# A decoder step on one core: another order of the opening and of the gates and values

## The chip, the cores and the metric

The kernel runs on one core of a Trainium2 chip. The metric is the device time of one execution in microseconds (us); each kernel is run several times and the median counts. A core has five engines that run their own instruction streams and wait for one another by semaphores: TensorE (PE, matmuls and transposes; PEld is its load of weights), VectorE (DVE), ScalarE (ACT), GpSimd (POOL) and SyncE (SP, which issues DMA transfers; ScalarE issues some too).

## The reference

One layer of a decoder, for 1024 prompt tokens and 8 sample tokens, 1032 columns in all, in float32:

```
h    = rmsnorm(x, norm_mix_g)
u, q, k, v, gate, f_low = split(h @ w_in)          # one projection
pool = grouped window means of u (2/4/8/16 tokens) minus u, a linear map, a scale
logf = log_sigmoid(f_low @ w_forget_up + b_forget) / 16
o    = gated linear attention(q, k, v, logf)       # 4 heads, chunks of 64
x    = x + concat(pool, rmsnorm(o) * silu(gate)) @ w_out
mk   = rmsnorm(mem) @ w_km;   mv = rmsnorm(mem) @ w_vm        # 256 memory tokens
x    = x + cross attention(rmsnorm(x), mk, mv) @ w_om
x    = x + square(relu(rmsnorm(x) @ w_up)) @ w_down
```

Its outputs are y, the last rows of u, the state of the attention, and mk and mv.

## The kernel before

Activations are held transposed, features on the partitions and tokens along the row, in chunks of 128 features x 1032 tokens. Each float32 operand of a large product is split into a high and a low part: ScalarE casts the high part (line 159, or 162 with a gain), VectorE or POOL subtracts for the low part (line 160, or 163 with a gain). A product is three matmuls per pair of tiles: high x high, high x low, low x high. A group of projection columns (128 of them) is 8 x 9 = 72 matmuls (gemm_chunk, line 196).

*The opening* (lines 286 to 415) computes the keys of the memory, mk, and prepares the tokens. It is a list of steps in three strings, START_A to START_C, of which each word calls a function with a number:

- m (mem_turn): transposes half of the memory tokens (ptm), multiplies them with a norm vector (mg) and splits them (mn).
- l (k_load): loads a block of 128 columns of w_km in two halves (wkm, 256 KB each) through three raw buffers, and splits them (wk).
- K (k_chunk): a key product, 24 matmuls into acck; e (k_scale) scales it into mkT; t (k_turn) transposes it back (ptk) for the output.
- x (x_load): loads a quarter of the prompt tokens (xt, 1 MB; the fifth is the sample tokens, xs); q (x_square) sums their squares on ScalarE.
- X (x_chunk): transposes a chunk of 128 features of all tokens (ptx), copies it (xT), stores it (xd) and splits it (h); f (f_part): its six matmuls for the low-rank gate (accf).
- S, R, N, r: the norms of the memory and the tokens; L: the gate's weights.

The words set the priority. A scheduler orders each engine's instructions, so that those of later words can pass earlier ones that wait. PSUM has two buffers of the pool mp (acck, ptm, ptk, ptg) and two of accp (ptx, accf, the projection's sums).

*The projection* follows: pool_in(3) (U, line 498, is its scaled copy), forget() (accz, line 465, then Z and Y on VectorE and ScalarE, scans, and decays), pool_in(2), pool_in(1), two groups each of keys and queries, and then gates (g, ge with a reciprocal on VectorE at line 574, gt), values (vt, line 586) and pool_in(0), written out one after the other. pool_win sums windows on POOL (W) and leaves pl on VectorE. Each group also adds pieces of w_down in pairs (ws, line 439), which are ready for the last part of the layer. After the projection comes the recurrence of the attention, again a list of steps: its first need the vt of the last values, kinv and qd; beside them run the products of w_vm (accv, line 732) and of the pooled channels (accp, line 531).

Lines named in the profile: 109 and 103 the gains (norm vectors, loaded as rows grow, transposed as ptg, copied to gcol), 160 splits, 303 the issue of wkm, 345 K, 362 and 364 X, 386 f.

## Time and profile before

| | us |
|---|---|
| times of the kernel before, three runs | 1379.63, 1381.21, 1384.13 |
| median | 1381.21 |
| profiled execution, its time | 1386.28 |
| profiled execution, its span | 1384.6 |

[...] The span begins with the first instruction; all times of rows count from there. The opening ends at about 66.5 us, the projection at about 260 us, and the recurrence follows.

How to read the rows: the page gives the busy time of each engine. In the table of stretches a row is the stretch (from:to in us) and its length, then for PE, PEld, DVE, ACT and POOL the busy us with the number of instructions, then the granted clock, the share of the DMA engines' time in use, and GB/s. In the order in time a row is the start, the duration of all instructions merged in it, the engine, the line, the operation, the tile written and those read, the shape and the count; a bracket gives the idle time of the engine before it and what ended that.

### The profile page before, as it was taken

How to read it: one execution, taken by the hardware profiler on the slowest of the kernel's cores; microseconds unless marked ns; L12 is line 12 of the kernel's file. 1: busy time of each engine (PE TensorE's matmuls, PEld its weight loads, DVE VectorE, ACT ScalarE, POOL GpSimd, SP SyncE). 2: the span in 40 equal slices, each digit the busy share in tenths (PEclk: the TensorE clock that was granted, in tenths of full speed). 3: DMA queues.
4: the chain of work that ended last, by engine and by line, in shares of the span. 5: the costliest groups of instructions: out<-in, count | busy, mean ns of one | idle time of the engine just before them, and what ended most of it. 6: DMA issues, size and time to landing. Idle time of an engine off the chain costs nothing.

```text
span 1384.6 us, 22609 instructions
## 1 busy us (share of the span) xinstructions
PE 1330.3 (96%) x8734; PEld 1237.2 (89%) x8734; DVE 924.0 (67%) x1490; ACT 578.9 (42%) x1060; POOL 135.3 (10%) x177
## 2 busy tenths in 40 slices
PE   7999999899999999999999999989999999989997
PEld 6999999888999999878977898989897999989887
DVE  5778565696555677873768488777867654675664
ACT  6522112355334343543557444445445433232432
POOL 2134100100012000002200011112110000000000
PEclk9999999999999999999999999999999999999999
DMA  7846553585465356565435556556649964986671
GB/s 255 254 142 175 147 148 110 153 251 170 134 193 183 99 176 221 176 226 162 132 116 167 173 192 200 184 169 207 199 163 377 302 214 159 286 245 189 214 223 67
DMA packets 287477, 261.38 MB, mean 189 GB/s; under 512 B 13416, under 2 KB 239602, under 8 KB 287241
## 3 DMA queue, kind: packets, MB, share of 16 engines
q1 hardware_dynamic: 275209, 226.08, 52.8%
q0 software_dynamic: 6400, 21.17, 4.0%
q10 hardware_dynamic: 5760, 12.68, 2.5%
q8 instruction: 68, 1.11, 0.3%
q14 instruction: 40, 0.33, 0.1%
HBM read 195.04 MB, written 64.85 MB: 188 GB/s over the span
## 4 chain that ended last, share of the span: by engine, by line
PE 78%; DVE 7%; DMA 6%; issue 4%; ACT 3%; SPq 0%; POOL 0%; DVEq 0%; ACTq 0%; POOLq 0%
PE acc L196 29%; PE accd L1282 20%; PE acc L1109 16%; PE accl L1282 2%; PE accpv L979 1%; PE acck L345 1%; PE accsc L956 1%; DMA fd<-c 1%; DMA fac<-fd 1%; PE accv L732 1%; DMA w<-in_w_up 1%; PE accg L661 1%; PE psv L913 1%; DMA vt<-in_cache_mem_v 1%; DMA wvm<-in_w_vm 1%
## 5 line engine op out<-in xcount | busy, mean ns | idle before, releaser
L1109 PE MATMUL acc<-T,wuph 128*128 128x260 f32 (+1 forms) x1408 | 290.3, 317 | 10.9 <-DVE c L1153 6.1
L1282 PE MATMUL accd<-F,wdnh 128*128 128x260 f32 (+1 forms) x1344 | 266.0, 310 | 4.5 <-ACT wdnh L159 4.5
L1109 PEld LDWEIGHTS acc<-T,wuph 128*128 128x128 f32 x1408 | 213.8, 190 | 32.1 <-issue 7.3
L1282 PEld LDWEIGHTS accd<-F,wdnh 128*128 128x128 f32 x1344 | 201.1, 189 | 18.5 <-ACT wdnh L159 4.9
L1109 PE MATMUL acc<-T,wupl 128*128 128x260 f32 (+1 forms) x704 | 180.1, 316 | 0.8 <-DVE wupl L160 0.8
L1282 PE MATMUL accd<-F,wdnl 128*128 128x260 f32 (+1 forms) x672 | 167.1, 311 | 3.4 <-DVE wdnl L160 3.4
L1109 PEld LDWEIGHTS acc<-T,wupl 128*128 128x128 f32 x704 | 117.2, 191 | 11.3 <-DVE wupl L160 2.1
L1282 PEld LDWEIGHTS accd<-F,wdnl 128*128 128x128 f32 x672 | 109.5, 189 | 11.6 <-DVE wdnl L160 4.9
L159 ACT CAST wdnh<-wdn 128x1024 fp32r<-128x1024 f32 x52 | 54.5, 1050 | 129.4 <-PE accd L1282 112.4
L196 PE MATMUL acc<-c,womh 128*128 128x260 f32 (+2 forms) x384 | 81.8, 322 | 0.6 <-ACT c L159 0.5
L160 DVE TENSOR_TENSOR wdnl<-wdn,wdnh 128x1024 fp32r<-128x1024 f32 x52 | 63.5, 1221 | 20.7 <-ACT wdnh L159 20.6
L160 DVE TENSOR_TENSOR F<-fac,F 128x1040 fp32r<-128x1040 f32 (+1 forms) x52 | 63.2, 1231 | 15.0 <-ACT F L159 13.2
L159 ACT CAST F<-fac 128x1040 fp32r<-128x1040 f32 (+1 forms) x52 | 54.5, 1056 | 44.7 <-DMA fac<-fd 37.3
L196 PE MATMUL acc<-hm,wqmh 128*128 128x344 f32 x384 | 72.7, 323 | 0.1
L196 PEld LDWEIGHTS acc<-c,womh 128*128 128x128 f32 x384 | 59.5, 188 | 6.6 <-ACT c L159 0.6
L159 ACT CAST wuph<-w 128x512 fp32r<-128x512 f32 x64 | 39.0, 614 | 56.8 <-PE acc L1109 48.2
L196 PEld LDWEIGHTS acc<-hm,wqmh 128*128 128x128 f32 x384 | 61.7, 188 | 1.1 <-DVE v L260 0.4
L1113 ACT ACTIVATE c<-c 128x512 f32<-128x512 f32 (+1 forms) x64 | 40.2, 629 | 51.1 <-DVE c L1163 37.4
L1272 DVE TENSOR_TENSOR wdn<-wdn 128x1024 f32<-128x1024 f32 x24 | 29.4, 1225 | 43.2 <-DMA wdn<-in_w_down 43.2
L160 DVE TENSOR_TENSOR wupl<-w,wuph 128x512 fp32r<-128x512 f32 x64 | 43.5, 688 | 17.6 <-ACT wuph L159 17.3
L196 PE MATMUL acc<-c,woml 128*128 128x260 f32 (+2 forms) x192 | 49.7, 320 | 0.3 <-DVE woml L160 0.3
L1026 POOL TENSOR_TENSOR ss<-ss,sq 128x512 f32<-128x512 f32 (+1 forms) x12 | 18.9, 1574 | 241.7 <-ACT sq L1024 241.7
(404 smaller groups left out, 2588.3 us busy)
## 6 DMA issues: line engine op xcount, KB each, us to landing
wdn<-in_w_down SPq DMA_DIRECT2D x64, 512.0 KB
fac<-fd SPq DMA_DIRECT2D x32, 520.0 KB
w<-in_w_up SPq DMA_DIRECT2D x64, 256.0 KB
ws<-in_w_down SPq DMA_DIRECT2D x48, 256.0 KB
fac<-fd SPq DMA_DIRECT2D x20, 512.0 KB
fd<-w POOLq DMA_DIRECT2D x32, 260.0 KB, 2.6
x<-xd SPq DMA_DIRECT2D x16, 516.0 KB
xd<-x SPq DMA_DIRECT2D x16, 516.0 KB
```

The lines of the kernel that those rows point to most:

```text
L159: A.copy(out=dst_hi, in_=src)
L160: (eng or V).tensor_tensor(out=dst_lo, in0=src, in1=f(dst_hi), op=ALU.subtract)
L196: PE.matmul(acc[:, g, :c1 - c0], w, X[k][j][:, c0:c1], start=(k == 0 and i == 0), stop=(k == len(W) - 1 and i == 2))
L345: PE.matmul(acc[:, 0, :MT], w[:, x, k, :], mn[y][:, k, :], start=(k == 0 and q == 0), stop=(k == KC - 1 and q == 2))
L661: PE.matmul(pss[:, 2 * p:2 * p + 2, :], kinv[:, p, cs], qz[:, p], start=True, stop=True)
L732: PE.matmul(acc[:, m, :], mn[x][:, k0 + kk, m * P:(m + 1) * P], y[:, kk, :], start=(k0 == 0 and kk == 0 and q == 0 and m == 0), stop=(k0 = ...
L913: PE.matmul(psv[:2 * NB, 0, :], pz[h % 2][:, bb + b, m, :], vs[:, j, b, m, :], start=(bb + b + m + j == 0), stop=(bb + b + m + j == NB + M ...
L1026: eng.tensor_tensor(out=ss2[:, cs], in0=ss2[:, cs], in1=sq, op=ALU.add)
L1109: PE.matmul(acc, w, t[k // 2][:, k % 2, j, c0:c1], start=(first and k == 0 and i == 0), stop=(k == HK - 1 and i == 2), skip_group_check=True)
L1113: A.activation(out=t, in_=t, func=AF.Relu)
L1272: V.tensor_tensor(out=raw[0], in0=raw[0], in1=raw[1], op=op)
L1282: PE.matmul(acc, W[x][:, k, :], ff[:, y, k % 2, c0:c1], start=(q == 0 and k == 0 and i == 0), stop=(q == 1 and k == UK - 1 and i == 2))
```

## The change

It has five parts.

1. The three strings of steps are written anew: the weight loads and key products come first, the token loads stand between the key products, and the squares and the chunks X1 to X7 come later.
2. The six loads of norm vectors other than the memory's are issued by ScalarE instead of SyncE, and their transpose and copy (gains_turn) come after START_B instead of before it.
3. Both halves of a key weight block are split by VectorE; before, the second was POOL's.
4. The sums of the key products 1 and 2 are in the PSUM pool accp instead of mp.
5. At the end of the projection the order is gates 0, values 0, gates 1, gates 2, values 1, gates 3, values 2, pool_in(0), values 3; before, it was gates 0, values 0, gates 1, values 1, pool_in(0), gates 2, values 2, gates 3, values 3.

Lines behind k_chunk stand three lower in the changed kernel (L364 is L367).

```diff
--- before.py
+++ after.py
@@ -43,10 +43,10 @@
 
 
 
-START_A = "m0 l1 m1 l0 x0 x1 x2"
-START_B = "l2 K0 S q0 R x3 K1 x4 K2 l3 e0 t0 e1 l4 L q1 e2 t1"
-START_C = ("q2 X0 X1 l5 K3 X2 X3 q4 f0 K4 K5 e3 e4 e5 l6 t2 X4 q3 f1 K6 t4 f2 N l7 K7 f3 f4 X5 e7 X6 f5 t3 t7 r f6 e6 "
-           "t5 X7 t6 f7")
+START_A = "m0 m1 l0 l1 l2 x0"
+START_B = "K0 S l3 x1 K1 R l4 K2 x2 K3 e0 e1 l5 x3"
+START_C = ("e2 K4 l6 x4 e3 q0 K5 t0 l7 e4 t1 K6 q1 e5 t2 K7 L q2 t3 e6 X0 q3 e7 X1 t4 X2 q4 N t5 f0 X3 f1 t6 X4 f2 t7 "
+           "X5 f3 r X6 f4 f5 X7 f6 f7")
 GLA = ("P0 m a0 P2 v b0 m n0 m P3 m m P1 o0 m a1 t0 a2 . b1 n1 . m b2 a3 . m n2 m s0 s1 . b3 o1 m ... t1 n3 m m . "
        "o2 a4 t2 b4 t3 . n4 m ... a5 o3 m b5 .... n5 a6 o4 b6 t4 t5 m . n6 . a7 x . m . b7 o5 ... n7 . o6 .... t6 "
        "o7 . t7 ...")
@@ -92,7 +92,7 @@
 
     gv = {}
 
-    def gains(*names):
+    def gains(*names, eng=SY):
 
         rows = [a[nm][0] if nm == "gla_norm_g" else a[nm][0].rearrange("(c p) -> c p", p=P) for nm in names]
         n = sum(r.shape[0] for r in rows)
@@ -100,7 +100,7 @@
         gcol = const.tile([P, n], F32, name="gcol" + names[0])
         i = 0
         for nm, r in zip(names, rows):
-            SY.dma_start(grow[i:i + r.shape[0]], r)
+            eng.dma_start(grow[i:i + r.shape[0]], r)
             gv[nm] = gcol[:, i:i + r.shape[0]]
             i += r.shape[0]
 
@@ -301,7 +301,7 @@
             ks = slice(4 * i, 4 * i + 4)
             raw = wp.tile([P, 4, P], F32, tag="raw", name="wkm", bufs=3)
             SY.dma_start(raw, src[:, ks])
-            split(w[:, 0, ks], w[:, 1, ks], raw, eng=(V, G)[i])
+            split(w[:, 0, ks], w[:, 1, ks], raw)
 
     def x_load(i):
         if i < 4:
@@ -338,7 +338,10 @@
             split(mn[0][:, k:k + 4, ms], mn[1][:, k:k + 4, ms], mg)
 
     def k_chunk(c):
-        acc = mp.tile([P, 2, MT], F32, tag="m", name="acck")
+        if c in (1, 2):
+            acc = accp.tile([P, BANKS, 512], F32, tag="acc", name="acck3")
+        else:
+            acc = mp.tile([P, 2, MT], F32, tag="m", name="acck")
         w = WK.pop(c)
         for k in range(KC):
             for q, (x, y) in enumerate(((0, 0), (0, 1), (1, 0))):
@@ -398,13 +401,13 @@
              't': k_turn, 'X': x_chunk, 'L': f_load, 'f': f_part, 'R': lambda: spread(rm, mr[:, 1, :], MT),
              'N': tokens_rsqrt, 'r': lambda: tokens_spread("r1")}
     run(START_A)
-    gains_turn = gains("norm_mix_g", "norm_mem_g", "norm_ffn_g", "b_forget", "pool_scale", "gla_norm_g")
-    gains_turn()
+    gains_turn = gains("norm_mix_g", "norm_mem_g", "norm_ffn_g", "b_forget", "pool_scale", "gla_norm_g", eng=A)
     g_mix, g_nm, g_ffn = gv["norm_mix_g"], gv["norm_mem_g"], gv["norm_ffn_g"]
     b_f, psc, g_gla = gv["b_forget"], gv["pool_scale"], gv["gla_norm_g"]
     mkT = slot([P, KC, MT], F32, "mkT")
     mk_tok = slot([P, MC, D], F32, "mk_tok")
     run(START_B)
+    gains_turn()
     run(START_C)
     acc = FW[KC]
     r1 = rr.pop()
@@ -617,14 +620,14 @@
     t = values(0)
     gates(1)
     values_turn(0, t)
+    gates(2)
     t = values(1)
+    gates(3)
+    values_turn(1, t)
+    t = values(2)
     U = pool_in(0)
-    values_turn(1, t)
+    values_turn(2, t)
     pool_win(0, U)
-    gates(2)
-    t = values(2)
-    gates(3)
-    values_turn(2, t)
     t = values(3)
```

How it moves the instructions, at three places. The first is VectorE in the opening before: splits of key weights (wk), scales of key products (mkT), copies of token chunks (xT) and their splits (h).

```order
L160 TENSOR_TENSOR wk<-wkm,wk 128x512
L160 TENSOR_TENSOR fw<-fraw,fw 128x4x16 x2
L350 TENSOR_TENSOR mkT<-acck,rm 128x256 x2
L160 TENSOR_TENSOR wk<-wkm,wk 128x512
L350 TENSOR_TENSOR mkT<-acck,rm 128x256
L364 COPY xT<-ptx 128x1032
L160 TENSOR_TENSOR wk<-wkm,wk 128x512
L364 COPY xT<-ptx 128x1032
L163 SCALAR_TENSOR_TENSOR h_375<-xT,gcolnorm_mix_g,h_375 128x1032
L350 TENSOR_TENSOR mkT<-acck,rm 128x256
L364 COPY xT<-ptx 128x1032
L163 SCALAR_TENSOR_TENSOR h_391<-xT,gcolnorm_mix_g,h_391 128x1032
```

In the changed kernel the same engine's rows from the tenth weight split on are these.

```order
L160 TENSOR_TENSOR wk<-wkm,wk 128x512
L353 TENSOR_TENSOR mkT<-acck,rm 128x256
L160 TENSOR_TENSOR wk<-wkm,wk 128x512 x3
L353 TENSOR_TENSOR mkT<-acck,rm 128x256
L160 TENSOR_TENSOR wk<-wkm,wk 128x512
L353 TENSOR_TENSOR mkT<-acck,rm 128x256
L160 TENSOR_TENSOR wk<-wkm,wk 128x512
L367 COPY xT<-ptx 128x1032
L160 TENSOR_TENSOR wk<-wkm,wk 128x512
L163 SCALAR_TENSOR_TENSOR h_539<-xT,gcolnorm_mix_g,h_539 128x1032
L353 TENSOR_TENSOR mkT<-acck,rm 128x256
L367 COPY xT<-ptx 128x1032 x2
```

The copies xT and the splits h stand behind nearly all of the weight splits and key scales, where before they stood between them.

The second is SyncE, the issue of the opening's loads, before:

```order
L103 DMA grow<-in_gla_norm_g 4x128
L309 DMA xt_186<-in_x_prompt 128x2x1024
L303 DMA wkm<-in_w_km 128x4x128
L309 DMA xt_188<-in_x_prompt 128x2x1024
L309 DMA xt_190<-in_x_prompt 128x2x1024
L303 DMA wkm<-in_w_km 128x4x128 x3
L374 DMA fraw<-in_w_in 128x8x16
L309 DMA xt_262<-in_x_prompt 128x2x1024
L312 DMA xs<-in_x_sample 8x1024
L303 DMA wkm<-in_w_km 128x4x128 x9
```

and after:

```order
L117 DMA mem<-in_mem_prompt 128x1024 x2
L303 DMA wkm<-in_w_km 128x4x128 x6
L309 DMA xt_195<-in_x_prompt 128x2x1024
L303 DMA wkm<-in_w_km 128x4x128 x3
L377 DMA fraw<-in_w_in 128x8x16
L309 DMA xt_252<-in_x_prompt 128x2x1024
L303 DMA wkm<-in_w_km 128x4x128
L309 DMA xt_321<-in_x_prompt 128x2x1024
L303 DMA wkm<-in_w_km 128x4x128 x3
L309 DMA xt_359<-in_x_prompt 128x2x1024
L303 DMA wkm<-in_w_km 128x4x128
L312 DMA xs<-in_x_sample 8x1024
L303 DMA wkm<-in_w_km 128x4x128 x2
```

Six halves of key weights are issued ahead of the first token tile, where three were before (they stand above the first fence's rows); the loads of norm vectors (grow) are gone from this queue, and the token tiles stand one by one between the weights.

The third is VectorE at the end of the projection before, from the last gate (g) to the last values (vt) and beyond.

```order
L571 TENSOR_TENSOR g<-acc,r_697 128x1032
L160 TENSOR_TENSOR wpooll<-wpool,wpoolh 128x512
L598 COPY misc<-ptvs 8x128
L574 RECIPROCAL ge<-ge 128x1032
L439 TENSOR_TENSOR ws<-ws 128x512 x4
L575 SCALAR_TENSOR_TENSOR gt_2070<-g,gcolnorm_mix_g,ge 128x1032
L439 TENSOR_TENSOR ws<-ws 128x512 x2
L586 TENSOR_TENSOR vt<-acc,r_697 128x1032
L524 COPY misc<-ptp 23x128
L160 TENSOR_TENSOR pr<-pl_793,pr 128x1032
L160 TENSOR_TENSOR wvml<-wvm,wvmh 128x512
```

After, from the last edit of pool_in(0)'s means (pl) on:

```order
L518 TENSOR_TENSOR pl_793<-pl_793,U 128x1
L442 TENSOR_TENSOR ws<-ws 128x512 x2
L160 TENSOR_TENSOR wvml<-wvm,wvmh 128x512
L442 TENSOR_TENSOR ws<-ws 128x512 x2
L589 TENSOR_TENSOR vt<-acc,r_678 128x1032
L527 COPY misc<-ptp 23x128
L160 TENSOR_TENSOR wvml<-wvm,wvmh 128x512
L527 COPY misc<-ptp 23x128
L160 TENSOR_TENSOR wvml<-wvm,wvmh 128x512
L442 TENSOR_TENSOR ws<-ws 128x512 x2
L160 TENSOR_TENSOR pr<-pl_793,pr 128x1032
L442 TENSOR_TENSOR ws<-ws 128x512 x2
```

The reciprocal of the last gate is no longer between the last value product and vt; four ws additions stand ahead of vt in the stretch, and others behind it.

## Rows read from the trace of the kernel before

**Rows 1.** The page, busy time of each engine: us, share, instructions.
```profile
PE 1330.3 (96%) x8734; PEld 1237.2 (89%) x8734; DVE 924.0 (67%) x1490; ACT 578.9 (42%) x1060; POOL 135.3 (10%) x177
```

**Rows 2.** The stretches of the opening, the projection and the recurrence (columns as told above).
```profile
12.00:20.00 8.00, 6.07 (x25) 5.55 (x26) 3.67 (x11) 6.42 (x16) 1.27 (x1) 1.00 1.04 396
20.00:30.00 10.00, 9.63 (x70) 9.26 (x69) 3.78 (x7) 6.06 (x15) 1.72 (x2) 1.00 0.96 254
30.00:40.00 10.00, 10.00 (x79) 9.41 (x80) 9.50 (x10) 6.53 (x10) 3.85 (x3) 1.00 0.71 242
...
81.00:88.00 7.00, 5.77 (x21) 5.54 (x21) 6.40 (x4) 0.53 (x1) 6.65 (x4) 0.51 0.93 254
...
112.00:252.00 140.00, 140.00 (x898) 139.27 (x897) 85.15 (x88) 26.46 (x38) 17.07 (x7) 1.00 0.50 145
...
260.00:264.00 4.00, 0.74 (x6) 0.56 (x5) 4.00 (x7) 0.00 (x0) 0.00 (x0) 1.00 0.85 319
264.00:269.00 5.00, 4.56 (x20) 4.08 (x20) 3.74 (x6) 1.25 (x2) 0.79 (x2) 0.66 0.22 68
269.00:276.00 7.00, 7.00 (x53) 6.13 (x52) 3.87 (x5) 4.50 (x7) 0.00 (x0) 1.00 0.28 80
276.00:304.00 28.00, 25.93 (x185) 23.00 (x184) 26.69 (x79) 18.91 (x64) 1.58 (x4) 1.00 0.78 232
```

**Rows 3.** The order in time on TensorE, opening: start, duration, instruction, idle time before.
```profile
13.38 3.01 PE L345 MATMUL acck<-mn,wk 128*128 128x256 f32 x12 [1.93 <-DVE mg L336]
...
26.50 3.05 PE L345 MATMUL acck<-mn,wk 128*128 128x256 f32 x24 [0.37 <-DVE mkT L350]
...
34.92 1.09 PE L362 MATMUL ptx<-ident,xt 128*128 128x128 f32 x8
...
65.90 0.64 PE L386 MATMUL accf<-h,fw 128*128 128x344 f32 x3
...
66.85 0.98 PE L602 MATMUL ptw<-selw,misc 120*128 120x8 f32 x8
```

**Rows 4.** The order in time on TensorE, pooling projection to key projection.
```profile
77.46 3.77 PE L465 MATMUL accz<-flow,misc 32*128 32x344 f32 x12
82.46 2.09 PE L196 MATMUL acc<-h,wuh 128*128 128x344 f32 x6 [1.23 <-DVE Z L466]
...
109.91 0.74 PE L196 MATMUL acc<-h,wkl 128*128 128x344 f32 x3 [1.14 <-DVE wkl L160]
```

**Rows 5.** The order in time on VectorE, first weight splits.
```profile
10.24 1.79 DVE L160 TENSOR_TENSOR wk<-wkm,wk 128x512 fp32r<-128x512 f32 x1
...
13.15 0.68 DVE L160 TENSOR_TENSOR wk<-wkm,wk 128x512 fp32r<-128x512 f32 x1
```

**Rows 6.** The order in time on POOL, its first weight split.
```profile
10.21 1.27 POOL L160 TENSOR_TENSOR wk<-wkm,wk 128x512 fp32r<-128x512 f32 x1 [7.12 <-ACT wk L159]
```

**Rows 7.** The order in time on SyncE, the fourth weight half.
```profile
11.51 0.39 SPq L303 DMA_DIRECT2D wkm<-in_w_km  x1
```

**Rows 8.** Groups of instructions of 0 to 70 us: count, busy, mean ns, idle.
```profile
L163 DVE SCALAR_TENSOR_TENSOR h<-xT,gcolnorm_mix_g,h 128x1032 fp32r<-128x1032 f32 x8 | 10.3, 1285 | 1.1 <-ACT h L162 1.0
...
L364 DVE COPY xT<-ptx 128x1032 f32<-128x1032 f32 x8 | 9.8, 1230 | 2.5 <-PE ptx L363 2.5
```

**Rows 9.** The order in time on VectorE, between the pooling groups.
```profile
77.57 1.23 DVE L498 TENSOR_TENSOR U<-acc,r 128x1032 f32<-128x1032 f32 x1 [4.73 <-PE acc L196]
...
89.72 1.21 DVE L512 SCALAR_TENSOR_TENSOR pl<-W,U 128x1009 f32<-128x1009 f32 x1 [2.28 <-POOL W L509]
```

**Rows 10.** The order in time on TensorE, end of the projection.
```profile
263.86 0.41 PE L657 MATMUL accg<-ident,kinv 128*128 128x128 f32 x2 [3.26 <-DVE vt L586]
```

**Rows 11.** The order in time on VectorE, end of the projection.
```profile
251.04 6.60 DVE L574 RECIPROCAL ge<-ge 128x1032 f32<-128x1032 f32 x1 [1.59 <-ACT ge L573]
257.56 2.60 DVE L439 TENSOR_TENSOR ws<-ws 128x512 f32<-128x512 f32 x4
...
262.50 1.22 DVE L586 TENSOR_TENSOR vt<-acc,r 128x1032 f32<-128x1032 f32 x1
```

## Prediction

> **What bounds the kernel now.** The shares of busy time come first: TensorE is busy 1330.3 us, 96 % of the span [rows 1]. So only two kinds of time can be won: the 4 % in which TensorE stands still, and stretches in which it works at half its clock. The table of stretches says where these lie in the parts that are edited [rows 2]. From 112 to 252 us TensorE is busy 140.00 of 140 us, so whatever is won before 112 us arrives undiminished at the end of the projection. [...]
>
> The order in time, with the releasers, names the waits. At the start the first key product is at 13.38 us [rows 3]. The pooling projection's second group of matmuls starts at 82.46 us after 1.23 us of idle time for Z on VectorE, behind 3.77 us of small accz products [rows 4]. At 109.91 us the key projection waits 1.14 us for VectorE's half of its weights [rows 4]. At 263.86 us TensorE has stood 3.26 us for vt [rows 10]. These are the places to follow; the profiled execution (1386.28 us, span 1384.6 us) is 5 us above the median of the runs, so I work out differences in it (the 1.7 us around its span stay) and take them from the median, 1381.21 us.
>
> **Opening, start.** In VectorE's order before, a weight split (wk, at 10.24 us) stands ahead of the third mn split and the fourth mg, and it took 1.79 us, while one like it at 13.15 us took 0.68 us [rows 5]; POOL's own wk split of 1.27 us began 0.03 us before it [rows 6]. The change gives POOL none of these splits and puts the fourth mg ahead of all wk splits. That is 1.1 us of stall and a 0.7 us split out of the way of the first key product, so it comes at about 11.5 us instead of 13.4 us. POOL's eight splits become eight times 0.68 us = 5.4 us on VectorE; they lie in the first 40 us, where VectorE waits for data, except the last two.
>
> **Opening, key products and loads.** A key product is 24 matmuls, 3.05 us with its tail [rows 3]. Three of them run back to back from 11.5 us, to about 20.5 us; before, the third ended at 29.5 us. The second and third now take their sums in the other PSUM pool, so none of them waits for a scale that is late. After that the loads set the pace. SyncE issues the fourth weight half only at 11.51 us [rows 7], when a split has given back one of the three raw buffers; that bound stays when the small vectors go to ScalarE's queue, so I count that edit as nothing (it costs at most the wait for its last vector, which the mixing gain needs only in the tail). From 11.5 us, 13 halves of 0.26 MB and four token tiles of 1.05 MB remain, 7.6 MB. At the 396 GB/s of 12 to 20 us this takes 19 us, at the 254 GB/s of 20 to 30 us 30 us [rows 2]: the last half lands between 31 and 42 us. I take 37 us, nearer to the slower row, because most of the stretch is weight halves behind three buffers. Squares now stand ahead of some casts on ScalarE; they are inside this spread.
>
> **Opening, tail.** The eight token chunks now come nearly all after the last weight splits. Each costs VectorE a copy xT of 1.23 us and an h split of 1.29 us [rows 8], 2.5 us less some overlap at the seams, say 2.4; TensorE needs eight transposes of 1.09 us in all and a short one [rows 3], 1.2 us, and six gate products of 0.156 us (140.00 us / 898 [rows 2]), 2.2 us. The store of each chunk, 128 x 1032 x 4 bytes, is 0.53 MB in 2.4 us, 220 GB/s, less than either rate above. So VectorE sets the pace: 8 x 2.4 = 19 us from 38 us (a cast and a split behind the last load), plus ten small diagonals and the last key scales, 3 us, plus the last gate product, 1 us: the gates end at about 61 us (57 to 64); before, at 66.5 us [rows 3]. Behind them stand 72 matmuls of the pooling projection. At 0.156 us these are 11.2 us; 0.9 us of window products (0.98 with their tail [rows 3]) and a third of accz, 1.3 us, stand inside: U can be copied out at 61 + 13.4 = 74.4 us instead of 77.57 us [rows 9], 3.1 us earlier.
>
> **Opening, what arrives.** Only four accz matmul rows (2.5 us) are left between the two pooling groups, and the Z for the first comes 1.2 us behind U, so the second group can start 3.2 us after U, before 4.9 us (82.46 - 77.57): TensorE itself is 4.8 us ahead there (3.1 + 4.9 - 3.2). But the chain from U to the key weights is not TensorE's: POOL's four W sums follow U, and pl waits for them until 89.72 us [rows 9]; from there to the weight split for which 109.91 us waits, VectorE's timeline has hardly a gap. This chain moves by U's shift: 2 to 4 us, I take 2.8, since a split or two may slip in. TensorE's surplus only lengthens the 1.14 us stall. **Opening: -2.8 us**, bounds +2 (the gates end at 64 us and the clock falls as before) and -4.1.
>
> **End of the projection.** Before, the reciprocal of the last gate, 6.60 us, four ws additions, gt and two more additions stand on VectorE ahead of the last vt [rows 11]. TensorE reaches the wait at 260.60 us (263.86 - 3.26); vt ends at 263.72. After, both gates are early, and only two ws pairs and a weight split stand ahead of vt; vt comes within 1.3 us of its matmuls, and TensorE has the last pooling channel and value products of the memory to do meanwhile. What goes: up to 3.26 us of wait [rows 10] and the half clock after it, some (1 - 0.66) x 5 = 1.7 us [rows 2]. What comes: six ws additions at 0.65 us (2.60 / 4), 3.9 us of VectorE [rows 11], move behind vt into the recurrence, where from 276 to 304 us VectorE is busy 26.69 of 28 us and TensorE 25.93 [rows 2]. Between 264 and 276 us VectorE has 1.26 + 3.13 = 4.4 us free [rows 2], which may hold them. From 0 (VectorE gives all of it back as waits in the recurrence) to -5.0; I take **-3.0 us**, since the gap at 264 to 276 us covers the additions but the early stages then meet a VectorE with no slack.
>
> **Sum.** -2.8 - 3.0 = -5.8 us: 1375.4 us.
>
> **Rivals.** [...]
>
> *Given back in the recurrence.* The wait at 263.86 us goes but reappears as waits on VectorE by 304 us. For it: 26.69 of 28 us there. Against: TensorE is busy 25.93, also nearly full. The opening alone, -2.8, gives 1378.4 us.
>
> *Both gains whole.* The half clock at 81 us does not come, VectorE's chain finds room, the recurrence takes the additions: -4.1 - 5.0 gives 1372.1 us. For it: the idle stretch before 82.46 us halves and the accz products are split up. Against: the chain through POOL does not depend on the clock.
>
> *The loads starve the keys.* Six weight halves stand ahead of the first token tile, and each half waits for one of three buffers whose split now waits behind squares on ScalarE and other work on VectorE. The last half lands at 42 us or later, the gates end at 65 to 67 us, as now, and the change of order does nothing; with the projection's half or none, 1379 to 1384, middle 1381.5 us.
>
> [...]
>
> **Chances.** Forecast (1375.4, own range 1373.5 to 1378) 0.38; given back in the recurrence 0.24; both whole 0.18; loads starve 0.12; clock falls 0.08. A difference under 0.3 % (4.1 us) can't be told from none here: faster is under 1377.1, slower over 1385.3. Faster: 0.34 of the forecast's, all of both whole (0.18), 0.03 of given back: 0.55. Same: 0.04, 0.19, and half of the starved case (0.06): 0.29. Slower: the clock (0.08), the other half of the starved case with other losses (0.06), 0.02: 0.16. The range runs from 1369.5 (both gains and a cheaper restart of the clock) to 1385.5.
>
> **What would show it.** Right: the first acck near 11.5 us and the third done by 21; a regular pitch of about 2.4 us of xT and h on VectorE from 37 us on, with TensorE waiting for h; U near 74.4 us; a longer stall than 1.14 us at wkl; no wait on vt, and the granted clock at 1.00 after the last values. Wrong: acck waiting for wkm until past 42 us; a clock under 1.00 between 42 and 62 us; or u in the recurrence no earlier against the last value product than before, with VectorE full from 260 to 304 us.

## The result and the profile after

| | before | after |
|---|---|---|
| median, us (11 runs each) | 1381.88 | 1393.22 |
| lowest to highest, us | 1378.77 to 1390.44 | 1388.43 to 1398.46 |
| profiled execution, time / span, us | 1386.28 / 1384.6 | 1394.98 / 1393.1 |

The ratio is 1.0073, with a 95 % interval of 1.0058 to 1.0089. The change makes the kernel 0.7 % slower; the forecast was faster (1375.4 us, range 1369.5 to 1385.5). The kernel before was run again beside each group of experiments, with medians from 1381.88 to 1383.63 us; each ratio below is against those runs. Two executions in the slow state, of 1615 and 3311 us (p5_copies_act and p18_squares_late), are left out of every number.

On the page after, beside [rows 1], TensorE is busy 5.0 us longer for as many instructions, and the span is 8.5 us longer. Both kinds of time that the prediction named have grown in the first 312 us: the mean granted clock there is 0.97 instead of 0.98, and TensorE's idle time 22.0 us instead of 18.6. Over the whole span the clock is 0.984 in both.

```profile
PE 1335.3 (96%) x8734; PEld 1237.1 (89%) x8734; DVE 921.9 (66%) x1498; ACT 578.2 (42%) x1060; POOL 127.0 (9%) x169
```

TensorE's order in time in the opening (beside [rows 3]; columns as there). The first key product comes at 10.51 us, and the first three, 72 of the 48 + 4 + 22 matmuls of the rows, run with nothing but two pairs of ptr between them, until 23.3 us. The key products are all done by 45 us. But the gates end at 68.28 us, after 66.54 before.

```profile
10.51 9.34 PE L348 MATMUL acck<-mn,wk 128*128 128x256 f32 x48 [1.12 <-ACT mn L159]
...
20.69 2.83 PE L348 MATMUL acck<-mn,wk 128*128 128x256 f32 x22
...
43.34 1.43 PE L348 MATMUL acck<-mn,wk 128*128 128x256 f32 x10
...
61.58 0.80 PE L244 MATMUL ptr<-dg,ones 128*128 128x128 f32 x4
62.31 0.33 PE L365 MATMUL ptx<-ident,xt 128*128 128x128 f32 x1
...
65.33 2.95 PE L389 MATMUL accf<-h,fw 128*128 128x344 f32 x9 [1.86 <-DVE h L163]
```

VectorE's order in time between the same points. The tail of copies xT and splits h starts at 41.34 us; its last copy waits 1.15 us for the transposes of the last chunk; the seventh split stands behind that copy, and TensorE's wait of 1.86 us ends with it; the last split begins at 65.46 us.

```profile
41.34 1.23 DVE L367 COPY xT<-ptx 128x1032 f32<-128x1032 f32 x1
...
61.24 0.44 DVE L242 TENSOR_SCALAR dg<-ident,tn 128x128 f32<-128x128 f32 x2 [0.51 <-PE ptr L244]
62.84 1.23 DVE L367 COPY xT<-ptx 128x1032 f32<-128x1032 f32 x1 [1.15 <-PE ptx L366]
63.98 1.28 DVE L163 SCALAR_TENSOR_TENSOR h<-xT,gcolnorm_mix_g,h 128x1032 fp32r<-128x1032 f32 x1
65.27 0.27 DVE L640 MEMSET misc<- 128x256 f32 x1
65.46 1.17 DVE L163 SCALAR_TENSOR_TENSOR h<-xT,gcolnorm_mix_g,h 128x1032 fp32r<-128x1032 f32 x1
```

The stretches of after (beside [rows 2]; the last three numbers are the granted clock as a share of full speed, the DMA share and GB/s). The half clock that stood at 81 to 88 us has moved: from 84 to 90 us the clock is now 1.00, and 64 to 76 us shows 0.64, 0.93 and 0.58. A second low stretch, 0.52, stands from 114 to 120 us (0.50 from 115 to 118 us), where before TensorE ran at 1.00. At 300 to 305 us there is a third, 0.66.

```profile
64.00:68.00 4.00, 2.67 (x9) 2.68 (x10) 2.63 (x4) 2.70 (x4) 0.00 (x0) 0.64 0.86 323
68.00:72.00 4.00, 4.00 (x21) 3.10 (x21) 3.47 (x7) 0.00 (x0) 0.00 (x0) 0.93 0.27 67
72.00:76.00 4.00, 4.00 (x17) 4.00 (x17) 1.83 (x5) 0.00 (x0) 0.00 (x0) 0.58 0.57 178
84.00:90.00 6.00, 5.45 (x27) 4.03 (x26) 5.97 (x6) 0.00 (x0) 4.62 (x3) 1.00 0.17 45
...
114.00:120.00 6.00, 6.00 (x22) 6.00 (x23) 4.33 (x10) 0.00 (x0) 1.56 (x1) 0.52 0.34 87
252.00:260.00 8.00, 8.00 (x55) 7.78 (x54) 5.27 (x8) 1.69 (x3) 2.21 (x1) 1.00 0.37 109
260.00:264.00 4.00, 4.00 (x28) 4.00 (x27) 1.90 (x3) 0.62 (x1) 0.44 (x1) 1.00 1.11 300
...
276.00:304.00 28.00, 21.77 (x136) 18.06 (x135) 20.98 (x42) 15.38 (x37) 1.08 (x3) 0.94 0.85 240
300.00:305.00 5.00, 4.70 (x23) 3.75 (x24) 3.26 (x10) 0.99 (x2) 0.66 (x2) 0.66 1.12 312
```

VectorE between the pooling groups (beside [rows 9]): U comes at 83.79 us instead of 77.57. The means pl follow at the old distance (12.1 us), TensorE's first matmul with the split key weights 30.05 us behind U, where it was 32.34. The second fence is TensorE, beside [rows 4]: the wait for wkl is 2.98 us, where it was 1.14.

```profile
83.79 1.23 DVE L501 TENSOR_TENSOR U<-acc,r 128x1032 f32<-128x1032 f32 x1 [4.79 <-PE acc L196]
...
95.92 1.21 DVE L515 SCALAR_TENSOR_TENSOR pl<-W,U 128x1009 f32<-128x1009 f32 x1 [4.27 <-POOL W L512]
...
111.42 2.37 DVE L160 TENSOR_TENSOR wkl<-wk,wkh 128x512 fp32r<-128x512 f32 x1
```

```profile
113.84 1.23 PE L196 MATMUL acc<-h,wkl 128*128 128x344 f32 x3 [2.98 <-DVE wkl L160]
```

The end of the projection on VectorE (beside [rows 11]): vt stands right behind its matmuls, and the wait of 3.26 us [rows 10] is gone. In its place VectorE stands at additions ws whose pieces of w_down have not landed, and pr, mp and the zb of the recurrence stand behind them in its queue.

```profile
264.88 1.49 DVE L442 TENSOR_TENSOR ws<-ws 128x512 f32<-128x512 f32 x2 [1.10 <-DMA ws<-in_w_down]
266.36 1.23 DVE L589 TENSOR_TENSOR vt<-acc,r 128x1032 f32<-128x1032 f32 x1
...
271.17 1.29 DVE L442 TENSOR_TENSOR ws<-ws 128x512 f32<-128x512 f32 x2 [1.99 <-DMA ws<-in_w_down]
272.38 1.23 DVE L160 TENSOR_TENSOR pr<-pl,pr 128x1032 fp32r<-128x1032 f32 x1
...
278.28 1.29 DVE L442 TENSOR_TENSOR ws<-ws 128x512 f32<-128x512 f32 x2 [1.72 <-DMA ws<-in_w_down]
279.61 1.29 DVE L163 SCALAR_TENSOR_TENSOR mp<-accp,gcolnorm_mix_g,mp 128x1032 fp32r<-128x1032 f32 x1
```

Two views sum this up. The waits of VectorE from 262 to 312 us (in total, how often, the longest) name the additions and a second late load, vb (the sample tokens' values, which come back from DRAM, vdr). TensorE's order in time shows who waits for the mp behind the additions, and for the split wvml behind vb.

```profile
DVE ws L442 <- DMA ws<-in_w_down: 7.7, 5, 2.6
DVE vb L760 <- DMA vb<-vdr: 3.6, 1, 3.6
```

```profile
281.05 0.71 PE L534 MATMUL accp<-pr,wpoolh 128*128 128x344 f32 x3 [1.82 <-DVE mp L163]
...
298.41 0.51 PE L735 MATMUL accv<-wvml,mn 128*128 128x256 f32 x2 [1.78 <-DVE wvml L160]
```

Two points in time serve as marks from here on. The first is the end of the last value product, taken at the end of its last row with wvh (three matmuls with wvl end about 0.5 us later, in every profile); the second is the first matmul with woh, behind the recurrence. Before:

```profile
258.21 1.11 PE L196 MATMUL acc<-h,wvh 128*128 128x344 f32 x6
...
301.25 1.22 PE L196 MATMUL acc<-mp,woh 128*128 128x344 f32 x6
```

After:

```profile
264.75 1.11 PE L196 MATMUL acc<-h,wvh 128*128 128x344 f32 x6
...
312.06 1.21 PE L196 MATMUL acc<-mp,woh 128*128 128x344 f32 x6
```

So the last value product ends 6.5 us later (265.86 against 259.32), and the first matmul with woh comes 10.8 us later.

### The profile page after: what moved, and what is told of

Read it like the earlier page. It is cut to its first block, busy times and chain, and to the rows that moved or that the text cites. A ratio compares the mean times of both kernels' runs of the same rounds, so it can differ in the third digit from the quotient of the medians.

```text
span 1393.1 us, 22605 instructions
## 1 busy us (share of the span) xinstructions
PE 1335.3 (96%) x8734; PEld 1237.1 (89%) x8734; DVE 921.9 (66%) x1498; ACT 578.2 (42%) x1060; POOL 127.0 (9%) x169
## 3 DMA queue, kind: packets, MB, share of 16 engines
q8 instruction: 68, 1.11, 0.3%
## 4 chain that ended last, share of the span: by engine, by line
PE 69%; DMA 11%; DVE 9%; issue 6%; ACT 2%; POOL 1%; SPq 1%; DVEq 0%; POOLq 0%; ACTq 0%
PE acc L196 28%; PE accd L1285 15%; PE acc L1112 13%; DMA wdn<-in_w_down 3%; PE accl L1285 2%; PE accpv L982 1%; PE acck L348 1%; DMA ws<-in_w_down 1%; PE accsc L959 1%; DMA w<-in_w_up 1%; DMA fd<-c 1%; DMA fac<-fd 1%; PE psv L916 1%; DVE wdn L1275 1%; PE accv L735 1%
## 5 line engine op out<-in xcount | busy, mean ns | idle before, releaser
L1285 PEld LDWEIGHTS accd<-F,wdnl 128*128 128x128 f32 x672 | 109.3, 188 | 11.5 <-DVE wdnl L160 4.6
L159 ACT CAST F<-fac 128x1040 fp32r<-128x1040 f32 (+1 forms) x52 | 54.4, 1056 | 42.8 <-DMA fac<-fd 34.2
```

The source lines that it names most:

```text
L159: A.copy(out=dst_hi, in_=src)
L1285: PE.matmul(acc, W[x][:, k, :], ff[:, y, k % 2, c0:c1], start=(q == 0 and k == 0 and i == 0), stop=(q == 1 and k == UK - 1 and i == 2))
```

## The experiments

The theory at the start (A): both halves lose. The opening costs 6 to 7 us, by a later end of the gates, a half clock behind it and a longer wait for wkl; the end of the projection costs about 4 us more, by additions that wait for their loads. In the cuts of code, lines are joined by semicolons and dots stand for what is left out.

**The two halves alone.** First the change without its part 5, then part 5 alone.

```diff
 p1_opening: the changed kernel with the old end of the projection
-    values_turn(0, t); gates(2); t = values(1); gates(3); ...
+    values_turn(0, t); t = values(1); U = pool_in(0); ...
```

> Only the opening of the change (steps, norm vectors, splits, PSUM pool); gates and values in the order of before. Theory A (the two halves of the change lose separately): the opening alone is 6 to 7 us slower than before, with the last value product about 6.5 us later than before, the gates done near 68 us, granted clock below 1 in 60 to 76 us and again behind the wait for wkl at about 114 us; the wait of 3.3 us for vt comes back. Rival B (the opening is harmless, its loss is only a chance of the profiled execution): within 3 us of before. Rival C (the halves lose only together): within 3 us of before here and in the run with the projection alone.

Measured: 1393.41 us, ratio 1.0067 [1.0043, 1.0092], some 9 us. The opening alone loses as much as the whole change, more than expected of it. Its last value product ends at 268.07 us; TensorE's wait for h ahead of the last gates is 1.85 us, that for wkl 2.99 us, and that for vt is back with 3.3 us.

```diff
 p2_projection: the kernel before with part 5 alone
-    values_turn(0, t); t = values(1); U = pool_in(0); ...
+    values_turn(0, t); gates(2); t = values(1); gates(3); ...
```

> Only the new order of gates, values and pool_in(0); the opening of before. Theory A: 4 us slower than before (2.5 to 5.5); vt follows its matmuls within 1 us, but VectorE then waits 5 to 8 us in all for the loads of ws in the 20 us behind it, and the first output product (mp,woh) comes about 4 us later against the last value product than before. Rival D (the additions wait for loads only because the slower opening has shifted the transfers): 2 to 4 us faster than before, with no wait of VectorE for ws over 1 us.

Measured: 1382.2 us, ratio 0.9985 [0.9968, 1.0002]: no change that can be told. The wait for vt is gone, and VectorE's waits show the same row as in the changed kernel:

```profile
DVE ws L439 <- DMA ws<-in_w_down: 7.9, 5, 3.1
DVE vb L757 <- DMA vb<-vdr: 2.4, 1, 2.4
```

So the additions that wait do not come from the late opening: the new order makes them. All ten profiles with part 5 have both rows (ws 7.0 to 8.5 us in five waits, vb 1.0 to 3.6 us in one), and none of the eight without it has either. They cost about what the vt wait did, not the 4 us more that was expected of them.

**The parts of the opening.** The splits come first, put back to POOL in the changed kernel, and moved to VectorE in the kernel before.

```diff
 p4_poolsplits: the changed kernel
-            split(w[:, 0, ks], w[:, 1, ks], raw)
+            split(w[:, 0, ks], w[:, 1, ks], raw, eng=(V, G)[i])
```

> The whole change, but the second half of each key weight block is split by POOL again. Theory A (VectorE waits for data while the keys run, and the tail begins only behind the last loads): within 2 us of the changed kernel, so 9 to 13 us slower than before. Rival E (the eight splits on VectorE make the tail late): 3 to 5 us faster than the changed kernel, 6 to 8 us slower than before, and the first xT 3 us or more earlier.

Measured: 1386.28 us, 1.0019 [0.9998, 1.0040]. The tail does not start earlier (first xT 42.98 us) and the gates end at 68.80 us; yet the wait for h is 0.69 us, the clock of 62 to 78 us is 1.00, and the last values end at 261.32 us. Neither theory holds: the gain of some 7 us on the changed kernel is more than the rival expected, and its sign, an earlier first xT, did not come. So a late end of the gates does not by itself give the loss.

```diff
 p11_splits_only: the kernel before
-            split(w[:, 0, ks], w[:, 1, ks], raw, eng=(V, G)[i])
+            split(w[:, 0, ks], w[:, 1, ks], raw)
```

> The kernel before with one edit: all key weight splits on VectorE. Theory G (the splits as such cost little, they only shift which instruction stands ahead of which in the tail): within 2 us of before, 1381 to 1385. Rival E (eight more splits on VectorE, 5.4 us, delay the copies and splits of the tokens): 4 to 7 us slower than before.

Measured: 1381.61 us, 0.9985 [0.9969, 1.0001]. In the old order the splits on VectorE cost nothing that can be told, as theory G said; what p4_poolsplits won by taking half of them away, it won in the new order alone.

**VectorE's tail.** The copies xT go to ScalarE, in the opening alone and in the whole change.

```diff
 p5_copies_act: p1_opening;  p10_change_copies: the changed kernel
-        V.tensor_copy(out=xT, ...)
+        A.copy(out=xT, ...)
```

> As the run of the opening alone, but the eight copies xT are made by ScalarE instead of VectorE. Theory A (VectorE's copy and split of 2.5 us per chunk set the pace of the tail): the pitch of a chunk falls from 2.57 us to about 2.3 us (ScalarE then has a copy and a cast), the gates are done 2 to 3 us earlier, near 65 to 66 us, and if the clock then does not fall the time is 3 to 6 us below the opening alone. Rival F (TensorE or the transposes set the pace): no change of the pitch, time within 1.5 us of the opening alone.

Measured: 1385.72 us, 1.0011 [0.9989, 1.0032]. The gain of 7 us is more than theory A said, and not by its way: from the first copy to the last the pitch of a chunk is 3.3 us, 3.1 in p1_opening, and the gates end later, at 69.14 us. But matmuls of the pooling projection stand between them; no wait for h is over 0.6 us, U comes at 78.89 us, and the last values end at 259.01 us.

> The whole change with the eight copies xT made by ScalarE. Theory G: no half clock at 64 to 76 us, as in the run of the opening alone with these copies; the wait for wkl under 1.5 us and no half clock behind it; last value product within 1 us of before; time 1380 to 1385 us, some 9 us below the change. Rival J (the recurrence's waits for ws in the new order of gates and values cost 3 us more behind any opening): 1386 to 1390 us.

Measured: 1388.73 us, 1.0044 [1.0029, 1.0059]. Its profile has U at 79.10 us, the clock at 1.00 in both stretches of the table below, a wait for wkl of 2.65 us, and the last values at 258.49 us, as early as in the kernel before. The median is nevertheless some 6 us up. The time is the one of rival J, but its mechanism does not show: from the last values to the first woh matmul it takes as long as in p5_copies_act (42.8 and 42.9 us). What is more than before lies behind that, and why stays open.

**The wait for h.** First it is filled with matmuls that nobody reads, then it is shortened by moving the norm step r behind the last chunk, then the squares are moved.

```diff
 p6_filler: p1_opening, in f_part
+        fill = {6: 10, 7: 6}.get(k, 0)
+        if fill:
+            pf = mp.tile([P, 2, MT], F32, tag="m", name="pfill")
+            for _ in range(fill):
+                PE.matmul(pf[:, 0, :MT], FW[k], H[k - 1][1][:, :MT], start=True, stop=True)
```

> As the run of the opening alone, with 16 extra matmuls of 128x256 whose results nobody reads, ten in the wait before the last three products of the seventh chunk's gate and six before those of the eighth (about 1.9 us of TensorE). Theory G (what costs is the clock that falls when TensorE waits 1.9 us for h there): the granted clock stays 1.00 from 62 to 78 us, U comes 2.5 to 4.5 us earlier than in the opening alone (86 us), near 82.5, and the time is 3 to 5 us below it although TensorE does more. Rival H (the clock falls for another reason, or the stall itself is what costs): the clock still falls, and the time is the same or up to 2 us above the opening alone.

Measured: 1388.81 us, 1.0043 [1.0027, 1.0060]. The clock is 1.00 up to 70 us; the half clock comes at 70 to 75 us instead (0.70 from 70 to 72 us, 0.50 from 72 to 74 us), and U at 82.83 us. U and the time (4.6 us below p1_opening) come out as theory G said, though the clock falls all the same: the fill goes with a later and shorter half clock and does not prevent it.

```diff
 p9_r_late: p1_opening
-           "X5 f3 r X6 f4 f5 X7 f6 f7")
+           "X5 f3 X6 f4 X7 f5 r f6 f7")
```

> As the run of the opening alone, but the spread of the token norms (step r, with its matmuls ptr) is written after X7 instead of before X6. Theory G (the eighth chunk's transposes stand on TensorE behind ptr, which waits for VectorE's diagonals; so xT, h and the gates come late, TensorE waits 1.9 us and the clock falls): no wait of over 1 us ahead of the last gates, clock 1.00 from 62 to 78 us, U 4 to 6 us earlier than in the opening alone, near 81 us, time 1385 to 1389 us. Rival I (VectorE's sum of copies and splits is the limit, whoever stands where): gates done within 1 us of the opening alone, U within 1.5 us, time within 2 us of it.

Measured: 1391.78 us, 1.0053 [1.0032, 1.0074], from 1385.12 to 1394.62. In its profile (1387.86 us) the step does what it was meant to: TensorE's longest wait for h is the row below, the gates end at 65.82 us, U comes at 80.13 us and the last values end at 259.56 us. So the profile is the one of theory G, but the median is the one of rival I, 1.6 us below p1_opening.

```profile
65.08 0.74 PE L389 MATMUL accf<-h,fw 128*128 128x344 f32 x3 [0.65 <-DVE h L163]
```

> The run with step r behind X7 a second time, for its profile alone: its first profile gained 8.5 us on the opening alone by the last value product, its median only 1.6 us. If executions differ in where the half clock falls, this profile shows it at 62 to 78 us or behind wkl, and the last value product 2 us or more later than 259.6 us. If it repeats the first within 1.5 us, the median's loss lies behind the projection.

Measured in the second profile, p15_r_late_again: 1387.07 us, the last values at 259.83 us, the first profile repeated. Both profiled executions lie 4 to 5 us below the median. What the others did differently no profile shows.

```diff
 p18_squares_late: p9_r_late, START_C
-... "e2 K4 l6 x4 e3 q0 K5 t0 l7 e4 t1 K6 q1 e5 t2 K7 L q2 t3 e6 X0 q3 e7 X1 ..."
+... "e2 K4 l6 x4 e3 K5 t0 l7 e4 t1 K6 e5 t2 K7 L t3 e6 X0 q0 e7 X1 q1 t4 X2 q2 ..."
```

> As the run with step r behind X7, and all squares of the tokens behind the last key product. Theory N (the casts of the key weights wait on ScalarE behind squares, which wait for token loads): the last key product ends 3 us or more earlier than there (44.6 us), by 41.5 us, the first xT begins by 39 us instead of 41.2, the gates are done by 64 us, U by 78.5 us instead of 80.1, and the time is 1 to 3 us below that run. Rival O (the loads set the pace, with or without squares): the last key product within 1.5 us of 44.6 us, U within 1 us of 80.1 us or later, since the squares now lie among the casts of the tail; time the same or above.

Measured: 1401.38 us, 1.0148 [1.0117, 1.0178]. The key products end at 44.22 us, where they ended at 44.60 us in p9_r_late: the squares on ScalarE did not hold them up. From 10 to 45 us ScalarE's casts now wait 10.7 us in nine waits for the loads of wkm (2.0 us in three in the changed kernel), so rival O holds. The squares now delay the norms; the gates end at 72.19 us and U comes at 86.94 us. The low clock stands at 56 to 62 us here (0.72), where TensorE is busy 4.22 of 6 us, and 62 to 78 us has 1.00.

**The wait for wkl.** The window sums of the first group go behind the second group's U, alone and with r late.

```diff
 p12_win_later: the changed kernel;  p13_both: also r late, as in p9_r_late
-    pool_win(3, U);  U = pool_in(2)
+    U3 = U;  U = pool_in(2);  pool_win(3, U3)
```

> The whole change with one edit more: the first window sums (pool_win(3)) are written after pool_in(2), so that Z, the scans and the first weight split of the keys stand ahead of pl on VectorE, which waits for POOL. Theory K (the chain from U over POOL's window sums and pl to wkl, 28.7 us in every run with the new opening, makes TensorE wait 3 us for wkl and sets off the half clock behind it): no wait for wkl over 0.5 us, clock 1.00 from 110 to 124 us, the key projection's second weight part 3 us earlier and the query projection 5 to 6 us earlier than in the change; time 1386 to 1389 us. Rival L (VectorE's other work takes the place of pl, and the wait stays): within 2 us of the change.

Measured: 1392.12 us, 1.0059 [1.0039, 1.0079]. The first split wkl is early (110.38 us, and takes 0.68 us), the clock of 112 to 120 us is 1.00, but a wait of 2.0 us comes at the second wkl, the tail still has its half clock (0.63 in 62 to 78 us), and the last values end at 268.61 us. Only half of theory K holds, and the time is the one of rival L.

> The whole change with both edits: the spread of the token norms behind X7, and the first window sums behind pool_in(2). Theory G and K together: no half clock from 62 to 78 us and none from 110 to 124 us, U near 80 us, last value product 6 us or more earlier than in the change, below 260 us; time 1379 to 1385 us, at or below the kernel before. Rival M (the half clock comes back at other places, the accz products or the recurrence): 1386 to 1390 us.

Measured: 1389.71 us, 1.0043 [1.0025, 1.0061], as rival M said; the clock is 1.00 from 62 to 78 us and 0.88 from 110 to 124 us, and the last values end at 262.08 us. Better than the change, still slower than before.

**The same kernel three times more.** The changed kernel was profiled again, since the medians and the profiles did not agree.

> The changed kernel a second time, for its profile alone. If the half clock at 65 to 75 us and at 114 to 120 us belongs to the kernel, both stand at the same places again and the last value product ends within 1.5 us of 265.9 us. If they come and go by execution, one is missing or elsewhere, and the last value product moves by 2.5 us or more.

> The changed kernel a third time, for its profile alone. If the half clock makes the difference between its executions: with a spell at 64 to 76 us the last value product ends at 263 to 268 us, without one at 260 to 261.5 us; the order of the instructions and the waits for h (1.9 us) and wkl stay as they are.

> The changed kernel a fourth time, as the third: with a spell at 64 to 76 us the last value product ends at 263 to 268 us, without one at 260 to 261.5 us.

Measured, with the profile of the result as the first of four:

| | first | p14 | p19 | p20 |
|---|---|---|---|---|
| time, us | 1394.98 | 1387.38 | 1389.90 | 1393.23 |
| gates end, us | 68.28 | 67.37 | 67.17 | 67.25 |
| clock 62 to 78 us | 0.79 | 1.00 | 0.68 | 0.68 |
| clock 84 to 90 us | 1.00 | 0.72 | 1.00 | 1.00 |
| U, us | 83.79 | 81.19 | 85.36 | 85.67 |
| first wkl matmul, us | 113.84 | 111.26 | 115.41 | 115.72 |
| last value product ends, us | 265.86 | 260.57 | 264.74 | 267.68 |

The rows of two of them, 62 to 78 and 84 to 90 us, first p14, then p20, show the half clock standing either at the one place or at the other:

```profile
62.00:78.00 16.00, 13.98 (x82) 12.36 (x82) 9.70 (x15) 3.98 (x7) 0.00 (x0) 1.00 0.65 206
84.00:90.00 6.00, 6.00 (x28) 5.60 (x27) 5.00 (x4) 0.93 (x1) 5.79 (x3) 0.72 0.64 167
```

```profile
62.00:78.00 16.00, 13.98 (x53) 11.45 (x53) 9.10 (x14) 3.22 (x6) 0.00 (x0) 0.68 0.64 202
84.00:90.00 6.00, 5.45 (x26) 3.79 (x25) 4.33 (x5) 0.62 (x1) 2.83 (x2) 1.00 0.01 3
```

TensorE is busy as long, with 82 matmuls in the first and 53 in the second. The three executions with the half clock ahead of U have their last values 4 to 7 us later than the one without, as was expected of p19 and p20. All four have a wait for h of 1.9 us, so the wait alone does not decide it.

**Two harmless parts together.** Part 5 and part 3 on the kernel before.

```diff
 p21_two_parts: p2_projection
-            split(w[:, 0, ks], w[:, 1, ks], raw, eng=(V, G)[i])
+            split(w[:, 0, ks], w[:, 1, ks], raw)
```

> The kernel before with two parts of the change, the new order of gates and values and all key weight splits on VectorE, and without its steps, norm vectors and PSUM pool. Theory P (the loss needs the new order of the steps, which puts all token chunks into one tail): no wait for h of over 1 us before the last gates, clock 1.00 from 62 to 78 us, time 1377 to 1381 us, at or below before. Rival Q (the parts only look harmless alone): 1385 to 1389 us.

Measured: 1384.21 us, 1.0003 [0.9987, 1.0018]. No change that can be told, neither the gain of theory P nor the loss of rival Q, and no half clock in 62 to 78 us (1.00). So the loss needs something of parts 1, 2 and 4. No run takes parts 2 and 4 (norm vectors and PSUM pool) apart from part 1, so that the new order of steps is what costs is argued, not shown; for it speaks that in the profile after the norm vectors' copy is done at 27.10 us, 14 us ahead of the first xT. No version here is told apart from the kernel before on the faster side.

## Why the prediction was wrong

*The start of the opening: right in its order.* The first acck was forecast at 11.5 us and came at 10.51; the third key product, forecast to end at 20.5 us, ended at 23.3. The term of 3.05 us for each product was too small: two stretches of one microsecond each in the profile after show 7 matmuls from 14 to 15 us and 11 from 18 to 19 us, both at a granted clock of 1.00 and with TensorE busy throughout. Why the pace differs, the rows do not show. The first row of [rows 3], 12 matmuls in 3.01 us, had shown the slow beginning, and was passed over.

```profile
14.00:15.00 1.00, 1.00 (x7) 1.00 (x6) 0.16 (x1) 0.77 (x4) 0.00 (x0) 1.00 1.04 310
...
18.00:19.00 1.00, 1.00 (x11) 1.00 (x10) 0.69 (x1) 0.15 (x1) 0.00 (x0) 1.00 0.97 370
```

*The tail of the opening: this step failed.* "The gates end at about 61 us (57 to 64)" was said; the four profiles give 67.2 to 68.3. The terms of the sum were mis-sized. The tail starts at 41.34 us, not 38. SyncE waited for the raw buffers of the weights to the end, as [rows 7] showed for the fourth half; that this alone sets the start is not shown. Its waits of 0 to 50 us have this row, the total, the count and the longest:

```profile
SPq L303 <- DVE wk L160: 12.1, 9, 3.7
```

And eight chunks plus what stands between them take 25.3 us (41.34 to 66.63), not 22. The copies of the fourth to sixth chunk start 2.6 us apart, near the forecast 2.4; the seventh comes 3.3 us and the eighth 5.1 us behind the one before. There the step r sends its diagonals through VectorE and its matmuls ptr through TensorE, among the transposes of the seventh and eighth chunks, so the last xT waits 1.15 us, and the seventh and last h with it. Moving r took 1.2 us off TensorE's wait for h and let the gates end 1.7 us earlier (p9_r_late against p1_opening). The prediction counted VectorE's work but not the handovers between the two engines. The last gate products took 1.65 us, not 1: 3.3 + 3.3 + 0.65 make the 7.3 us from 61 to 68.28.

*From the gates to U: right, with one thing missing.* The sum said U comes 13.4 us behind the gates. In p14, whose clock is 1.00 from 62 to 78 us, it is 81.19 - 67.37 = 13.8 us. In the other three it is 15.5, 18.2 and 18.4 us: the half clock falls into this stretch. So of the 9.6 us by which U misses its forecast on average (84.0 against 74.4), 6.5 lie at the gates (67.5 against 61) and 3.1 behind them. The sum itself says that gates later than 77.57 - 13.4 = 64.2 us lose, because the pooling projection now stands behind the gates where part of it ran beside them. But the gates' end alone does not order the runs: p4_poolsplits and p5_copies_act end theirs at 68.80 and 69.14 us, later than any profile of the change, and lose least of the new openings; there U comes 13.2 and 9.8 us behind, with the clock at 1.00.

*The half clock: the sign was foreseen, the place was not.* A fall of the clock had a chance of 0.08 and was looked for between 42 and 62 us, where transposes and products alternate. There the clock stayed 1.00 (42 to 62 us in the profile of after, 46 to 62 us in the three others of the changed kernel). It fell behind that, at 64 to 76 us. The stretches of all profiles taken together:

| profiles | clock 62 to 78 us | clock 84 to 90 us | U, us |
|---|---|---|---|
| old opening: before, p2, p11, p21 | 1.00 in all | 0.68, 0.88, 0.83, 0.82 | 77.57, 76.41, 77.67, 77.80 |
| new, wait for h 1.9 us: after, p19, p20, p1, p12 | 0.79, 0.68, 0.68, 0.57, 0.63 | 1.00, 1.00, 1.00, 1.00, 0.99 | 83.79, 85.36, 85.67, 86.03, 87.13 |
| the same wait: p14 | 1.00 | 0.72 | 81.19 |
| new, wait for h under 0.7 us: p4, p5, p9, p15, p13 | 1.00 in all | 0.72, 0.63, 0.75, 0.56, 0.72 | 82.02, 78.89, 80.13, 80.01, 80.60 |

Each of these has one low stretch in the one place or the other; of the rest, p6_filler has it in between (70 to 75 us), p18 ahead of both, and p10 nowhere here. In the old opening it lies behind U's matmuls, beside POOL's W sums (81.37 to 89.68 us in the profile before). In that profile the key weights are late there (1.14 us), which can hide a part of it; p2, p11 and p21 have no such wait, and what it costs there no run shows. In the new opening it mostly lies ahead of U, and U's delay goes through to the last values. That the wait for h moves it is an association over these profiles (5 of 6 with the long wait, none of 5 with the short one), not shown as a cause; p14 speaks against the wait alone, and so does p6_filler, whose wait was filled.

*The chain behind U: right.* "This chain moves by U's shift": the start of POOL's first sum to the end of wkl took 28.6 us in the profile of after (85.17 to 113.79) and 30.9 before (78.94 to 109.85). Averaged over the four profiles of each opening, U is 6.6 us later, the first wkl matmul 6.0 and the last value product 7.3 (264.71 against 257.41). So TensorE's full stretch from 112 us passes on what it gets, as argued from [rows 2], but what it got was a loss. In the first profile, p1 and p20 a second low stretch follows the wait for wkl (0.57, 0.70 and 0.67 from 112 to 120 us); in p19, p6_filler and p18, with waits of 3.0, 3.0 and 2.9 us, it does not (1.00 there, in p18 up to 124 us).

*The end of the projection: this step failed too; the rival "given back in the recurrence" was right for this half.* The forecast of -3.0 us counted six ws additions as 3.9 us of work and found room for it. It did not ask when their data land. Between 252 and 260 us the DMA engines are used at 0.37 (109 GB/s); then everything comes at once, 1.11 of 260 to 264 us. In the rows pr, mp and zb start only when the addition ahead of them on VectorE, which waited for a load, is over. From the last value product to the first woh matmul it is 41.9 us before, 43.6 in p2, and 46.2, 44.2, 43.8 and 42.4 in the four profiles of after, although the wait for vt, which lay in this stretch, is gone. In time, p2 alone does not exclude the -3.0 us (its interval reaches to -0.32 %); but the kernel with part 5 is not faster in any of three other pairs (p21 beside p11, the change beside p1, p10 beside p5).

*What stays open.* Of the 10 us of the ratio, 7.3 are there at the last values and 8.8 at the first woh matmul (308.9 against 300.0 us, the same four profiles of each opening). From there to the end the profiles take 1079 to 1086 us with the new opening and 1077 to 1083 with the old one, too spread to tell a difference. Why p9, p10 and p13 have medians 5 to 8 us above before although the last values of their profiles are only 1 to 5 us later than 257.41, no run settles. So the mechanism is shown for the profiled executions, and for the medians only in part.

## What to carry to other kernels

A product moved early pays only if what it was moved past does not become the tail: work out the new tail's end with the handovers between its engines, not with the busy time of the fullest one, and compare it with the point at which it would break even. Ask of each low-clock stretch whether it lies on the path; where it came ahead of another engine's chain here and not beside it, the same kernel was later by 4 to 7 us at the last values. An instruction whose data may be late should not stand, on its engine, ahead of work that the next stage needs: here three additions ws held VectorE for 1.10, 1.99 and 1.72 us, with vt, pr and mp behind them.

## What the hardware showed that was not expected

The granted clock of the same kernel's same stretch differs between executions: 1.00, 0.79, 0.68 and 0.68 from 62 to 78 us, with gates ending within 1.1 us of each other. Four profiles, and not one, told what the change does.

The first split wkl took 2.37 us at 111.42 us, begun while POOL was at a W sum (a row of two sums, 4.80 us from 110.76 us), and 0.67 us in the kernel before, at 109.18 us, when POOL's sums were over (103.88 + 4.57 = 108.45). In p12_win_later it took 0.68 us, at 110.38 us, although POOL was busy with two instructions for 1.92 of the 2 us from 110 to 112 us. What makes the split long no run isolates. The same split took 2.38 us in p11_splits_only, in the old opening, so it is no effect of the change alone.
